# Dilated attention in an encoder layer: k copied on chip, statistics moved to VectorE, the join of head pairs placed later

## The chip, the cores and the metric

The kernel runs on one core of one Trainium2 chip. The metric is the device time of one execution in microseconds. Engines go by the profile's names: PE (TensorE, the matrix engine), DVE (VectorE), ACT (ScalarE), POOL (GpSimd) and SP (SyncE, which here issues the DMAs).

## The reference

One encoder layer, float32, run for a prompt of 256 tokens and a sample of 1024 tokens with shared weights:

```python
x = x + 0.5 * rms_norm(swiglu(rms_norm(x, g1), w_gu, w_down), g2)
x = x + rms_norm(mixer(rms_norm(x, g3)), g4)
x = x + 0.5 * rms_norm(swiglu(...))     # second feed-forward
x = rms_norm(x, final_g)

# mixer: [q|k|v|ga|gb] = h @ w_in, 8 heads of 64
outs, lses = [], []
for window, dilation in ((128, 1), (512, 4), (2048, 16)):
    o, lse = dilated_branch(q, k, v, slopes, dilation, window // (2 * dilation))
    outs.append(o); lses.append(lse)
w = softmax(stack(lses), axis=0)
attn = sum(w[..., None] * stack(outs), axis=0)
c = silu(layer_norm(depthwise_conv31(ga * sigmoid(gb))))
return concatenate([attn, c]) @ w_out
```

## The kernel before

Matrix products work on pairs (hi, lo): a value is rounded to float32r, and the rest is kept as a second tile. The program runs the first feed-forward, the mixer's input projection `w_in` with the convolution, the attention, the output projection `w_out`, and the second feed-forward. The projection writes q, k and v to DRAM (`qd`, `kd`, `vd`), and `attn` loads them head by head. `qd` and `kd` hold a hi and a lo part; a tile `q` has hi in partitions 0 to 63 and lo in 64 to 127, so k has to stand twice: `kH` and `kL` each hold the same 64 rows in both halves, loaded by four DMAs per head (L802). Buffers for q, k, v are two; heads alternate.

A head has nine groups (`qk_group`, two 128 x 256 blocks of scores each): four "classes" (tokens 4i + c of the sample, c = 0 to 3, which carry the branches of dilation 4 and 16), the prompt (group 4), and four of the near band of the sample, for which q is rearranged by `cast_qb` on POOL (L807). For each block DVE adds a table and takes the row minimum (L858), ACT takes the exponential and the row sum (L864); both go into the statistics tile `st` ("ast"). `next_tab` scales the tables for the next head (L823 on DVE, L825 on POOL). `t_group` transposes the probabilities on PE (L935), `evac` copies them out of the PSUM banks on ACT or DVE (L931, L929), and `pv_group` multiplies by v (L963). The score blocks, the transposes and the small products share four PSUM banks.

The class part and the band part of the sample are then merged by their statistics:

- `merge1` gathers the class statistics into the band's layout: 16 copies of 32 x 4 values on POOL (L884), from one quarter of the partitions to another.
- `merge2` takes the common minimum (L892 to L894, DVE), `merge3` exponentials (L897, ACT), `merge4` the factors (L902 to L907, DVE).
- `merge5` transposes the factors (L912), writes them to DRAM (`fd`, L917) and reads them back broadcast over 64 partitions (`x`, L924): four DMAs on SP.
- After each odd head, two heads are joined: `combine1` multiplies both parts (`t`: tiles "to" or "tmp") by the factors on POOL (L1013), and `combine2` adds them: POOL writes the rounded sum to `hT` (L1022), then DVE writes the sum over one of the inputs (L1023) and takes the rest (L1024).
- The prompt's result is rounded by ACT (L984), its rest taken by DVE (L985).

The loop's index `i` runs over all (head, group) pairs; `when(k, g, f)` calls f(h) k steps after group g of head h. Transposes lag four steps behind the scores and products with v two more. The order in which Python issues instructions is their priority; the framework then orders each engine's instructions itself from a model of when they become ready, so one that is issued later may stand earlier in an engine's queue. Each engine works through its queue in order, SP's queue of DMAs too.

The last two steps of the attention already fetch and round the weights of `w_out`, whose products (tiles `pso`) follow; L206 to L212 are the first steps of the norm after them.

Of the kernel before, what the change touches and what calls it, by code (L numbers as in the profile page):

```python
# [10 lines left out]
F32 = mybir.dt.float32  # L11
F32R = mybir.dt.float32r
AF = mybir.ActivationFunctionType
# [15 lines left out]
NH = 8  # L29
HD = 64  # L30
# [118 lines left out]
class Trunk:  # L149
# [624 lines left out]
    def attn(self, qk, pool, rpool, qd, kd, vd, after):  # L774
        nc = self.nc
        mm = nc.tensor.matmul
        H = {}

        KW = 288
        bufs = []  # L780
        for i in range(2):
            q = qk[i].tile([P, NT], F32R, name=f"q{i}")
            qb = qk[i].tile([P, NS], F32R, name=f"qb{i}")
            k = [qk[i].tile([P, 5, KW], F32R, name=f"k{z}{i}") for z in "HL"]
# [10 lines left out]
        def load_qk(h):  # L795
            d = H.setdefault(h, {})
            q, qb, k, d["v"] = bufs[h % 2]
            f = slice(h * HD, (h + 1) * HD)
            for i in range(2):
                nc.sync.dma_start(q[i * HD:(i + 1) * HD].bitcast(F32), qd[i, f, :])  # L800
            for z, o, s in ((0, 0, 0), (0, HD, 0), (1, 0, 1), (1, HD, 1)):
                nc.sync.dma_start(k[z][o:o + HD, :, 16:16 + 256].bitcast(F32), kd[s, f, :].rearrange("f (c i) -> f c i", c=5))  # L802
            d["q"], d["qb"], d["k"] = q, qb, k

        def cast_qb(h):
            q, qb = bufs[h % 2][0:2]
            nc.gpsimd.tensor_copy(qb.rearrange("p (b c j) -> p b c j", b=8, c=4),  # L807
                                  q[:, 0:NS].rearrange("p (c b j) -> p b c j", b=8, c=4).bitcast(F32))

        def load_v(h):  # L810
            o = h % 2 * HD
            v = bufs[h % 2][3][:, :, o:o + HD]
            vh = vd[:, :, h * HD:(h + 1) * HD]
            for c in range(5):
                nc.sync.dma_start(v[:, 2 * c:2 * c + 2, :], vh[c, 16:272, :].rearrange("(b p) d -> p b d", p=P))
            for c in range(4):
                nc.sync.dma_start(v[c * 32:(c + 1) * 32, 10:19, :], vh[c].rearrange("(j i) d -> i j d", i=32))
# [60 lines left out]
        def merge1(h):  # L878
            d = H[h]
            d["X"] = pool.tile([P, 8, 2], F32, name="ax", tag="ax", bufs=2)  # L880
            x = d["X"].rearrange("p (h r) s -> p h r s", h=2)
            for c in range(4):
                for r in range(4):
                    nc.gpsimd.tensor_copy(x[c * 32:(c + 1) * 32, :, r, :],  # L884
                                          d["st"][r * 32:(r + 1) * 32, 4 * c:4 * c + 4].rearrange("p (h s) -> p h s", s=2))

        def merge2(h):
            d = H[h]
            y = d["y"] = pool.tile([P, 4, 8], F32, name="ay", tag="ay", bufs=2)
            z = d["B"] = d["st"][:, 20:36].rearrange("p (b s) -> p b s", s=2)  # L890
            v = nc.vector.tensor_tensor
            v(y[:, 3], d["X"][:, :, 0], z[:, :, 0], op=OP.min)  # L892
            v(y[:, 0], y[:, 3], d["X"][:, :, 0], op=OP.subtract)
            v(y[:, 1], y[:, 3], z[:, :, 0], op=OP.subtract)  # L894
# [47 lines left out]
        def t_group(h, g):  # L942
            d = H[h]
            ps = self.bank("pst")
            k = GROUPS[g]
            if g < 5:
                for kb in range(2):
                    for i in range(2):
                        tr(ps, kb * 256 + i * P, d["P"][2 * g + i][:, kb * P:(kb + 1) * P])
            elif g == 6:  # L950
                tr(ps, 0, band(h, 6, 1))
                tr(ps, P, band(h, 6, 0))
                tr(ps, 256, band(h, 0, 0))
                tr(ps, 384, band(h, 8, 1))
            else:
                for i, j in enumerate(k):
                    tr(ps, i * 256, band(h, j, 1))
                    tr(ps, i * 256 + P, band(h, j, 0))
            d["T", g] = evac(g, ps)


        def pv(out, d, blk, T, c0, n, first, last):
            mm(out, d["v"][:, blk, :], T[:, c0:c0 + n], start=bool(first), stop=bool(last))  # L963

        def pv_group(h, g):
            d = H[h]
            T = d.pop(("T", g))
            kt, odd = divmod(h, 2)
            if g < 4:
                if g == 0:  # L970
                    d["OB"] = H[h - 1]["OB"] if odd else self.two_banks("ob")
                out = d["OB"][:, g * 256:(g + 1) * 256]
                for kb in range(2):
                    pv(out, d, 2 * g + kb, T, kb * 256, 256, not odd and g % 2 == 0 and kb == 0, odd and g % 2 == 1 and kb == 1)
                if g == 3 and odd:
                    d["t"] = [pool.tile([P, NS], F32, name="to", tag="to", bufs=2) if h % 4 == 1 else self.tmp("tmp") for _ in range(2)]
                    nc.scalar.activation(d["t"][1], d["OB"], AF.Copy)
            elif g == 4:
                o = slice(odd * HD, (odd + 1) * HD)
                op = self.bank("op")[:, 0:256]  # L980
                for kb in range(2):
                    pv(op, d, 8 + kb, T, kb * 256, 256, kb == 0, kb == 1)
                hi, lo = (z[o, kt, :] for z in self.hT[2])
                nc.scalar.activation(hi, op[o], AF.Copy)  # L984
                nc.vector.tensor_tensor(lo, op[o], hi.bitcast(F32), op=OP.subtract)  # L985
            else:
                if g == 5:
                    d["OA"] = H[h - 1]["OA"] if odd else self.two_banks("oa")
                oa = d["OA"]

                def two(j, c0):
                    a, z = (j - 1) * P, (j + 1) * P
                    if j == 4:
                        pv(oa[:, a:a + P], d, 10 + j, T, c0, P, False, False)
                        pv(oa[:, a + P:z], d, 10 + j, T, c0 + P, P, not odd, False)
                    else:
                        pv(oa[:, a:z], d, 10 + j, T, c0, 256, not odd and j == 2, odd and j in (3, 7))
                if g == 6:
                    two(6, 0)
                    pv(oa[:, 0:P], d, 10, T, 256, P, False, False)  # L1000
                    pv(oa[:, 7 * P:8 * P], d, 18, T, 384, P, False, False)
                else:
                    for i, j in enumerate(GROUPS[g]):
                        two(j, i * 256)
                if g == 8 and odd:
                    nc.scalar.activation(d["t"][0].rearrange("p (c b j) -> p c b j", c=4, b=8),
                                         oa.rearrange("p (b c j) -> p c b j", b=8, c=4), AF.Copy)
# [7 lines left out]
        def combine2(h):  # L1015
            d = H[h]
            if h % 2:
                ta, tb = d["t"]
                for t in range(2):
                    c = slice(t * 512, (t + 1) * 512)  # L1020
                    hi, lo = (z[:, h // 2, :] for z in self.hT[t])
                    nc.gpsimd.tensor_tensor(hi, ta[:, c], tb[:, c], op=OP.add)  # L1022
                    nc.vector.tensor_tensor(ta[:, c], ta[:, c], tb[:, c], op=OP.add)  # L1023
                    nc.vector.tensor_tensor(lo, ta[:, c], hi.bitcast(F32), op=OP.subtract)  # L1024

# [3 lines left out]
        load_v(0)  # L1029
        load_qk(1)  # L1030
        load_v(1)
        cast_qb(0)
        cast_qb(1)

        def at(i):
            return seq[i] if 0 <= i < len(seq) else (-1, -1)

        for i in range(len(seq) + LAG + LAG2 + 11):
            def when(k, g, f):
                h, gg = at(i - k)  # L1040
                if gg == g and h >= 0:
                    f(h)

            hq, gq = at(i)
            ht, gt = at(i - LAG)
            hv, gv = at(i - LAG - LAG2)
            if ht >= 0:
                t_group(ht, gt)
            when(5, 8, merge5)
            when(3, 8, merge3)  # L1050
            if hq >= 0:
                qk_group(hq, gq)
            when(2, 4, prompt_norm)
            when(1, 8, merge1)
            when(2, 8, merge2)
            when(4, 8, merge4)
            when(8, 8, lambda h: cast_qb(h + 2) if h + 2 < NH else None)
            when(13, 8, combine2)
            if hv >= 0:
                pv_group(hv, gv)  # L1060
                if gv == 8 and hv + 2 < NH:
                    load_v(hv + 2)
            if hq >= 0:
                exp_group(hq, gq)
                after.get((hq, gq), lambda: None)()
            when(10, 8, combine1)


    def w_out(self, S, base, stages, new_hT):
# [247 lines left out]
```

## Time and profile before

| | |
|---|---|
| median of three runs | 2363.11 us (2356.36 to 2365.82) |
| the profiled execution | 2363.5 us, its span 2361.7 us |
| mean granted PE clock | 0.987 |
| busy: PE, weight loads, DVE, ACT, POOL | 2287.1, 1958.5, 1277.8, 809.4, 674.1 us |
| the attention loop (first to last product of scores) | 1199.5 to 1348 us |

A row of a timeline gives the start in us, the duration in us, the engine, the line, the operation, what it writes and reads, and in brackets for how long the engine was idle before it and what ended that. A row of a group of instructions gives busy us and the mean in ns, then the idle time before them and what ended most of it. A row of windows gives the stretch, its length, busy us of PE, weight loads, DVE, ACT and POOL with counts, then the granted clock, the DMA share and GB/s.

### The profile page before, as it was taken

How to read it: one execution, taken by the hardware profiler on the slowest of the kernel's cores; microseconds unless marked ns; L12 is line 12 of the kernel's file. 1: busy time of each engine (PE TensorE's matmuls, PEld its weight loads, DVE VectorE, ACT ScalarE, POOL GpSimd, SP SyncE). 2: the span in 40 equal slices, each digit the busy share in tenths (PEclk: the TensorE clock that was granted, in tenths of full speed). 3: DMA queues.
4: the chain of work that ended last, by engine and by line, in shares of the span. 5: the costliest groups of instructions: out<-in, count | busy, mean ns of one | idle time of the engine just before them, and what ended most of it. 6: DMA issues, size and time to landing. Idle time of an engine off the chain costs nothing.

```text
span 2361.7 us, 30596 instructions
## 1 busy us (share of the span) xinstructions
PE 2287.1 (97%) x11788; PEld 1958.5 (83%) x11788; DVE 1277.8 (54%) x1796; ACT 809.4 (34%) x1530; POOL 674.1 (29%) x702
## 2 busy tenths in 40 slices
PE   7999999999999999999998999999999999999996
PEld 6888888888788887888887878888888888788885
DVE  5744343444454567998466833834444444545457
ACT  4322222223221234665377722322222222312123
POOL 2332232321000034897125443223233232000004
PEclk8999999999999999999999999999999999999998
DMA  4222212214332333341279642122221222423224
GB/s 158 63 64 63 79 63 70 76 59 130 96 100 79 104 111 125 96 117 49 97 162 173 159 132 98 52 79 63 70 72 63 70 76 77 156 74 94 85 80 154
DMA packets 209240, 223.51 MB, mean 95 GB/s; under 512 B 31012, under 2 KB 161060, under 8 KB 209094
## 3 DMA queue, kind: packets, MB, share of 16 engines
q1 hardware_dynamic: 209094, 221.56, 31.6%
q8 instruction: 92, 1.51, 0.3%
q14 instruction: 54, 0.44, 0.1%
HBM read 163.52 MB, written 58.00 MB: 94 GB/s over the span
## 4 chain that ended last, share of the span: by engine, by line
PE 88%; DVE 3%; DMA 3%; issue 2%; ACT 2%; POOL 2%; SPq 0%; POOLq 0%; ACTq 0%; DVEq 0%
PE psAB L198 8%; PE psAB L199 8%; PE psAB L200 8%; PE psd L198 7%; PE psd L199 7%; PE psd L200 7%; PE psR L199 3%; PE psR L200 3%; PE psR L198 3%; PE psC L198 3%; PE psC L199 3%; PE psC L200 3%; PE psgu L198 2%; PE psgu L199 2%; PE psgu L200 2%
## 5 line engine op out<-in xcount | busy, mean ns | idle before, releaser
L115 DVE TENSOR_TENSOR wb<-raw,wb 128x512 fp32r<-128x512 f32 x240 | 167.2, 698 | 218.6 <-ACT wb L114 213.9
L114 ACT ACTIVATE wb<-raw 128x512 fp32r<-128x512 f32 x240 | 150.7, 629 | 325.4 <-PE psAB L200 134.9
L207 POOL TENSOR_SCALAR st<-st 128x1 f32<-128x1 f32 x70 | 40.9, 584 | 638.0 <-ACT tmp L206 364.7
L198 PE MATMUL psd<-wd,ahl 128*128 128x512 f32 x500 | 197.6, 395 | 9.4 <-ACT y L563 3.8
L452 POOL TENSOR_TENSOR ac<-ac,tmp 128x512 f32<-128x512 f32 x40 | 67.4, 1685 | 464.0 <-DVE tmp L448 452.6
L199 PE MATMUL psd<-wd,ahl 128*128 128x512 f32 x500 | 196.0, 392 | 0.0
L200 PE MATMUL psd<-wd,ahl 128*128 128x512 f32 x500 | 195.9, 392 | 0.0
L534 ACT ACTIVATE ahl<-ar 128x512 fp32r<-128x512 f32 (+1 forms) x132 | 72.9, 556 | 351.8 <-PE psd L200 251.5
L199 PE MATMUL psR<-hT2l,wb 128*128 128x256 f32 x640 | 181.1, 283 | 0.0
L200 PE MATMUL psR<-hT2h,wb 128*128 128x256 f32 x640 | 180.9, 283 | 0.0
L198 PE MATMUL psR<-hT2h,wb 128*128 128x256 f32 x640 | 180.5, 282 | 0.0
L114 ACT ACTIVATE wb<-g 128x512 fp32r<-128x512 f32 x80 | 50.6, 632 | 224.9 <-POOL g L136 96.5
L198 PEld LDWEIGHTS psR<-hT2h,wb 128*128 128x128 f32 x640 | 122.2, 191 | 6.1
L199 PEld LDWEIGHTS psR<-hT2l,wb 128*128 128x128 f32 x640 | 122.2, 191 | 4.7
L198 PE MATMUL psAB<-hT0h,wb 128*128 128x512 f32 x320 | 125.7, 393 | 0.0
L198 PE MATMUL psC<-hT1h,wb 128*128 128x512 f32 x320 | 125.5, 392 | 0.0
L199 PE MATMUL psAB<-hT0l,wb 128*128 128x512 f32 x320 | 125.5, 392 | 0.0
L199 PE MATMUL psC<-hT1l,wb 128*128 128x512 f32 x320 | 125.4, 392 | 0.0
L200 PE MATMUL psAB<-hT0h,wb 128*128 128x512 f32 x320 | 124.5, 389 | 0.0
L200 PE MATMUL psC<-hT1h,wb 128*128 128x512 f32 x320 | 124.5, 389 | 0.0
L565 DVE TENSOR_TENSOR y<-y,psd 128x1024 f32<-128x1024 f32 x70 | 85.3, 1219 | 71.2 <-PE psd L200 71.2
L200 PEld LDWEIGHTS psR<-hT2h,wb 128*128 128x128 f32 x640 | 122.2, 191 | 1.6
(388 smaller groups left out, 6284.9 us busy)
## 6 DMA issues: line engine op xcount, KB each, us to landing
raw<-in_ffn_w_gu_dram SPq DMA_DIRECT2D x88, 512.0 KB
ad<-ac SPq DMA_DIRECT2D x88, 256.0 KB
g<-in_ffn_w_down_dram SPq DMA_DIRECT2D x44, 512.0 KB
ar<-ad SPq DMA_DIRECT2D x88, 256.0 KB
raw<-in_w_in_dram SPq DMA_DIRECT2D x20, 512.0 KB
ar<-ad SPq DMA_DIRECT2D x44, 128.0 KB
ad<-x SPq DMA_DIRECT2D x40, 128.0 KB
x2d<-y SPq DMA_DIRECT2D x10, 512.0 KB
```

The costliest lines, as they stand in the source:

```text
L114: nc.scalar.activation(out[:, 0], src, AF.Copy)
L115: nc.vector.tensor_tensor(out[:, 1], src, out[:, 0].bitcast(F32), op=OP.subtract)
L198: mm(out, lh[0], rh[0], start=first, stop=False, skip_group_check=more)
L199: mm(out, lh[0], rh[1], start=False, stop=False, skip_group_check=more)
L200: mm(out, lh[1], rh[0], start=False, stop=last, skip_group_check=more)
L207: nc.gpsimd.tensor_scalar(st[:, 0:1], st[:, 0:1], 1e-6 / (mul * mul), None, op0=OP.add)
L452: nc.gpsimd.tensor_tensor(a1, a1, q, op=OP.mult)
L534: nc.scalar.activation(hl[0], r, AF.Copy)
L565: nc.vector.tensor_tensor(y[b], y[b], o, op=OP.add)
```

## The change

Five things are edited, all inside `attn`. k's hi and lo are loaded into the lower 64 partitions only, by two DMAs instead of four, and the new `double_k` copies them to the upper 64 on POOL, just ahead of the same head's `cast_qb`. The copies of `merge1` go to DVE, and are issued one step later, together with `merge2`. The rounding of the prompt's result goes from ACT to DVE. `merge5` is issued one step later. `combine1` comes at 11 steps instead of 10; `combine2` is cut in two: the POOL part comes at 14 steps instead of 13, the DVE part (`combine3`) at 17. For the last head the three stay at 10, 13 and 13.

```diff
-            for z, o, s in ((0, 0, 0), (0, HD, 0), (1, 0, 1), (1, HD, 1)):
-                nc.sync.dma_start(k[z][o:o + HD, :, 16:16 + 256].bitcast(F32), kd[s, f, :].rearrange("f (c i) -> f c i", c=5))
+            for z in range(2):
+                nc.sync.dma_start(k[z][0:HD, :, 16:16 + 256].bitcast(F32), kd[z, f, :].rearrange("f (c i) -> f c i", c=5))
...
+        def double_k(h):
+            for z in bufs[h % 2][2]:
+                nc.gpsimd.tensor_copy(z[HD:, :, 16:16 + 256], z[0:HD, :, 16:16 + 256].bitcast(F32))
...
         def merge1(h):
...
-                    nc.gpsimd.tensor_copy(x[c * 32:(c + 1) * 32, :, r, :],
+                    nc.vector.tensor_copy(x[c * 32:(c + 1) * 32, :, r, :],
...
-                nc.scalar.activation(hi, op[o], AF.Copy)
+                nc.vector.tensor_copy(hi, op[o])
                 nc.vector.tensor_tensor(lo, op[o], hi.bitcast(F32), op=OP.subtract)
...
                     nc.gpsimd.tensor_tensor(hi, ta[:, c], tb[:, c], op=OP.add)
+
+        def combine3(h):
+            if h % 2:
+                ta, tb = H[h]["t"]
+                for t in range(2):
+                    c = slice(t * 512, (t + 1) * 512)
+                    hi, lo = (z[:, h // 2, :] for z in self.hT[t])
                     nc.vector.tensor_tensor(ta[:, c], ta[:, c], tb[:, c], op=OP.add)
                     nc.vector.tensor_tensor(lo, ta[:, c], hi.bitcast(F32), op=OP.subtract)
...
+        double_k(0)
         cast_qb(0)
+        double_k(1)
         cast_qb(1)
...
+            def late(k, k_last, f):
+                for lag, hs in ((k, range(NH - 1)), (k_last, (NH - 1,))):
+                    h, gg = at(i - lag)
+                    if gg == 8 and h in hs:
+                        f(h)
...
-            when(5, 8, merge5)
+            when(6, 8, merge5)
...
-            when(1, 8, merge1)
-            when(2, 8, merge2)
+            when(2, 8, lambda h: (merge1(h), merge2(h)))
             when(4, 8, merge4)
-            when(8, 8, lambda h: cast_qb(h + 2) if h + 2 < NH else None)
-            when(13, 8, combine2)
+            when(8, 8, lambda h: (double_k(h + 2), cast_qb(h + 2)) if h + 2 < NH else None)
+            late(14, 13, combine2)
+            late(17, 13, combine3)
...
-            when(10, 8, combine1)
+            late(11, 10, combine1)
```

## The prediction

> **What bounds the kernel now.** I read the page's busy lines first, then the chain of waits through the attention stage, then the timelines of single engines there.
>
> ```profile
> span 2361.7 us, 30596 instructions
> PE 2287.1 (97%) x11788; PEld 1958.5 (83%) x11788; DVE 1277.8 (54%) x1796; ACT 809.4 (34%) x1530; POOL 674.1 (29%) x702
> PE 88%; DVE 3%; DMA 3%; issue 2%; ACT 2%; POOL 2%; SPq 0%; POOLq 0%; ACTq 0%; DVEq 0%
> ```
>
> The matrix engine (PE) sets the time: only its gaps can be won. The change touches nothing outside the attention loop, so I measure that loop by a mark that comes once a head: the first product of a head's prompt group, heads 1 to 7.
>
> ```profile
> 1226.59 0.47 PE L853 MATMUL pss<-kH,q 128*128 128x256 f32 x1
> 1242.81 0.47 PE L853 MATMUL pss<-kH,q 128*128 128x256 f32 x1
> 1258.96 0.47 PE L853 MATMUL pss<-kH,q 128*128 128x256 f32 x1
> 1284.16 0.47 PE L853 MATMUL pss<-kH,q 128*128 128x256 f32 x1
> 1302.27 0.47 PE L853 MATMUL pss<-kH,q 128*128 128x256 f32 x1
> 1319.59 0.47 PE L853 MATMUL pss<-kH,q 128*128 128x256 f32 x1
> 1341.41 0.47 PE L853 MATMUL pss<-kH,q 128*128 128x256 f32 x1
> ```
>
> The distances are 16.2, 16.2, 25.2, 18.1, 17.3 and 21.8 us. The first two heads run without a gap: 16.2 us a head, 1.80 us for each of its nine steps. The others lose 9.0, 1.9, 1.1 and 5.6: together 17.6 us. That is all that the loop's middle can give back, 0.75% of the time. Where the two large losses come from:
>
> ```profile
> 1245.22 1.74 SPq L917 DMA_DIRECT2D fd<-asb  x2
> 1255.61 4.70 POOL L1013 TENSOR_TENSOR to<-to,x 128x1024 f32<-128x1024 f32 x2 [7.45 <-DMA x<-fd]
> 1262.34 1.05 POOL L807 CAST qb<-q 128x1024 fp32r<-128x1024 f32 x1
> 1263.35 1.27 POOL L1022 TENSOR_TENSOR hT0h<-to 128x512 fp32r<-128x512 f32 x1
> 1264.65 1.73 DVE L1023 TENSOR_TENSOR to<-to 128x512 f32<-128x512 f32 x1 [6.80 <-POOL hT0h L1022]
> 1267.13 0.58 PE L853 MATMUL pss<-kH,qb 128*128 128x256 f32 x1 [5.12 <-DVE ast L858]
> 1265.00:1270.00 5.00, 2.87 (x11) 2.69 (x12) 5.00 (x13) 2.87 (x9) 4.51 (x14) 0.57 0.70 121
> ```
>
> First loss: the join of heads 0 and 1. GpSimd (POOL) waits for the factors (x from fd), multiplies (L1013), and only then adds (L1022). VectorE (DVE) had its own add L1023 next in its queue; it rewrites what L1022 reads and so waited 6.80 us, with the score minima of the next groups behind it. PE ran out of free score banks for 5.12 us, and then (last row, a 5 us window; its last three numbers are granted clock, DMA share and GB/s) got a clock of 0.57.
>
> ```profile
> 1327.58 4.66 POOL L1013 TENSOR_TENSOR to<-to,x 128x1024 f32<-128x1024 f32 x2 [5.74 <-issue]
> 1327.65 2.32 DVE L892 TENSOR_TENSOR ay<-ax,ast 128x8 f32<-128x8 f32 x1
> 1330.01 2.26 DVE L893 TENSOR_TENSOR ay<-ay,ax 128x8 f32<-128x8 f32 x1
> 1333.13 1.33 PE L963 MATMUL op<-pT,v 128*128 128x256 f32 x4 [3.79 <-ACT pT L931]
> 1332.21 2.13 POOL L825 TENSOR_SCALAR g<-g 128x768 f32<-128x768 f32 x1
> 1332.96 0.16 DVE L902 TENSOR_TENSOR ay<-ax,ay 128x8 f32<-128x8 f32 x1
> 1292.42 2.26 DVE L893 TENSOR_TENSOR ay<-ay,ax 128x8 f32<-128x8 f32 x1
> 1295.36 1.64 DVE L902 TENSOR_TENSOR ay<-ax,ay 128x8 f32<-128x8 f32 x1
> 1268.90 0.68 DVE L1023 TENSOR_TENSOR to<-to 128x512 f32<-128x512 f32 x1
> ```
>
> Second loss, and the small ones: VectorE's tiny adds of the statistics take 0.16 us, but 2.3 us each while GpSimd runs L1013. ScalarE's exponential (L897) waits for them, the copies pT queue behind it, and PE waits 3.79 us. So two-input work on both engines excludes itself. L902 at 1332.96 ran at its plain 0.16 under GpSimd's one-input L825.
>
> **The change, part by part.** How VectorE's delay becomes PE's loss I take from the three cases: 3.6 us of excess (1292 to 1297) cost 1.9, 4.3 (1327 to 1332) cost 5.6, 7.9 (6.80, and L1023's 1.73 against the 0.68 of its other half) cost 9.0. Some 2.5 us are free, the rest costs 1 to 2 us for each.
>
> *Later join.* Combine3 comes four steps later than L1023 did, 7.2 us. VectorE reached L1023 at 1257.85 (1264.65 - 6.80) and would reach it at 1265.05. GpSimd's L1022 ended at 1264.62. It moves by +1.8 (merge5, whose four DMAs bring the factors, and combine1 are one step later) and by +2.6 if the two new copies of k stand ahead of it as the cast L807 does: 1269.0. Against that stands the lighter DMA queue: from fd's issue to L1013 it is 10.4 us here, but 7.3 in the next pair:
>
> ```profile
> 1284.96 0.65 SPq L917 DMA_DIRECT2D fd<-asb  x2
> 1292.29 4.69 POOL L1013 TENSOR_TENSOR tmp<-tmp,x 128x1024 f32<-128x1024 f32 x2 [7.54 <-issue]
> ```
>
> so 0 to 3.1 us come back, and VectorE waits 0.9 to 4.0 us. I take 2.0, as half of k's traffic goes; with 1.1 for its own blocked add that is 3.1, costing 1.5. Of the 9.0, 7.5 are won (bounds 3 and 9). In the later pairs L1023 hardly waited, and four steps keep it so.
>
> *Multiplications a step later.* In pairs 3 and 5 L1013 starts about 1.8 us later against merge1 to merge4. It leaves merge2 and lands on merge4, whose six small operations follow merge2 within 3 us. The loss of 1.9, 1.1 and 5.6 (8.7 with rounding) can vanish, or both pairs can be hit like the second (11.3 + 1.1, a loss of 3.7 more). No row decides; I take the half, 4.4 won (-3.7 to 8.7).
>
> *Statistics on VectorE; ScalarE's copy.*
>
> ```profile
> L884 POOL COPY ax<-ast 32x4 f32<-32x4 f32 x128 | 31.2, 244 | 13.7 <-ACT pr L864 8.9
> L858 DVE CUSTOM_DVE_ANT_0 pr<-pss,g 128x256 f32<-128x256 f32 x144 | 55.2, 419 | 24.7 <-PE pss L854 24.4
> L984 ACT ACTIVATE hT2h<-op 64x256 fp32r<-64x256 f32 x8 | 3.0, 372 | 0.1
> L807 POOL CAST qb<-q 128x1024 fp32r<-128x1024 f32 x7 | 7.3, 1041 | 24.4 <-DMA q<-qd 21.7 <-PE psm L912 2.7
> L825 POOL TENSOR_SCALAR g<-g 128x768 f32<-128x768 f32 x7 | 15.0, 2141 | 7.9 <-DVE ast L858 7.9
> ```
>
> 16 copies a head leave GpSimd (3.9 us) and come to VectorE. No such copy runs there now; between 0.08 (back to back, half of L902's plain 0.16) and 0.244 each, it is 1.3 to 3.9 us a head. I take the 0.16: 2.6. The prompt copy of L984 adds about 0.35. Against these 2.9 stand VectorE's 24.4 / 8 = 3.1 us a head of waiting for PE. Cover enough, but not always in the right place: 0.2 a head, over 7 heads 1.5 lost (0 to 8.4, from (4.3 - 3.1) x 7). If the cover is gone, each microsecond costs one on PE.
>
> *k loaded once.* Per head two DMAs less (64 x 1280 x 4 bytes, 320 KB each), two GpSimd copies of 64 x 1280 more. By L807's rate one is 1.30 us; by L825's, 3.56. The first is a copy too, so I take 2.6 a head. The price is hidden if k stands before the head's first product. Head 7 (its loads, and its first product):
>
> ```profile
> 1308.82 1.09 SPq L800 DMA_DIRECT2D q<-qd  x2
> 1313.81 1.82 SPq L802 DMA_DIRECT2D kL<-kd  x2
> 1315.25 1.04 POOL L807 CAST qb<-q 128x1024 fp32r<-128x1024 f32 x1 [7.25 <-DMA q<-qd]
> 1327.59 0.36 PE L853 MATMUL pss<-kH,q 128*128 128x256 f32 x1
> ```
>
> q took 6.4 us to land; k, issued by 1315.63, lands near 1322.0, is doubled by 1324.6, and is needed at 1327.59: 3.0 us to spare. With the dear copies (7.1) it is 1.5 late. Head 4's loads of q and k queue on SP behind the postponed factors, up to 1.8 later, with two issues fewer ahead of the end; it needs the relief of the queue to be in time. Cost 0 (to 9, at 1.5 for six heads); queued behind a late copy on GpSimd are the cast L807, L825 and the joins.
>
> The first use, head 1, waits today:
>
> ```profile
> 1218.69 0.38 PE L854 MATMUL pss<-kL,q 128*128 128x256 f32 x1 [1.82 <-DMA kL<-kd]
> 1215.00:1220.00 5.00, 3.18 (x26) 2.85 (x25) 2.39 (x10) 2.62 (x10) 2.17 (x1) 1.00 1.24 195
> ```
>
> 0.64 MB less at 195 GB/s brings k 3.2 us earlier, the two copies take 2.6: 0 (2.2 won to 2.6 lost, from the copies alone).
>
> *Tail.* Only merge5 of head 7 moves, one step, with its four DMAs on SP; combine1 to 3 keep their place.
>
> ```profile
> 1379.21 1.28 DVE L212 SCALAR_TENSOR_TENSOR tmp<-pso,st,g 128x1024 f32<-128x1024 f32 x1 [1.70 <-POOL st L208]
> ```
>
> VectorE has 1.70 us idle before L212, which PE awaits next; 0.5 lost (0 to 1.8).
>
> *Sum.* 7.5 + 4.4 - 1.5 - 0.5 = 9.9 us. The profiled execution took 2363.5 (2361.7 and 1.8 around it), so 2353.6; its time is 0.4 above the median of the three runs, 2363.11. I predict 2353, 0.4% less.
>
> **The Trainium skill** ("SBUF — State Buffer", section "Who interferes with whom") says that GpSimd and VectorE share one port pair as an exclusive lock, which a VectorE copy in a two-port mode, or one with two SBUF inputs against a GpSimd reader, holds or waits for whole. L892 under L1013 agrees; L902, at 0.16 under the reading L825, does not. By that rule the sixteen copies meet every GpSimd instruction, and the result is the third rival.
>
> **Rivals.** *Everything goes.* The multiplications fall between the small adds and the join never waits: 2363.5 - 17.6 + 0.5 = 2346. For it: GpSimd sheds 3.9 us a head, and the queue is lighter. Against: L1013 still needs 4.7 us per pair, beside eight two-input operations of VectorE a head.
>
> *The join's wait stays.* GpSimd's adds come as late as VectorE's: the 9.0 are lost again, the rest as forecast: 2363.5 - 4.4 + 1.5 + 0.5 = 2361. For it: L807 stood ahead of L1022 already, and the copies of k may too. Against: 7.2 us of postponement exceed the 6.80.
>
> *Slower: VectorE becomes the loop's bound.* If each of its copies can be shut out by one-input GpSimd work, the two copies of k, L807 and L825 (2.6 + 1.04 + 2.14 = 5.8 us a head) delay it by half of that on average, 2.9. With 2.9 of own work and 3.1 idle, that is 2.7 x 7 = 19 lost, against 11.4 won elsewhere: 2371. It decides from 4.7 us of added VectorE time a head (3.1 + 11.4 / 7). For it: the 2.3 us adds; no VectorE copy lies under such an instruction now, so nothing excludes it. Against: L902.
>
> *Slower: k doubled late*, as priced: 9 us over six heads, with the copies ahead of the joins taking the 7.5 too: 2370.
>
> **Chances.** Forecast 0.42 (2348 to 2358), everything goes 0.26, the wait stays 0.20, VectorE bound 0.09, k late 0.03. About 0.5% (11.8 us) is what a measurement here tells from no change: faster means under 2351.3, all of the second case and a quarter of the first, 0.36; slower 0.12; the same 0.52. The range 2343 to 2367 leaves out the slower cases and a little on each side; the forecast's own is 2348 to 2358.
>
> **What would show it.** Right: marks 16.2 to 18 us apart throughout; no wait of L1023's successor above 3 us; the sixteen copies near 0.16 us each; no wait of L853 or L854 for GpSimd's k; the clock not below 0.9 in the middle. Wrong: a mark distance above 20, copies of 0.3 us and more beside GpSimd rows, PE waiting for k, or VectorE without idle time before L858.

## The result, and the profile after

The changed kernel takes 2384.27 us (median, 2381.62 to 2385.65) against 2362.44 for the kernel before: ratio 1.0094, 95% interval [1.0071, 1.0117]. It is 21.8 us slower; 2353 was forecast. First the page of the changed kernel: span, busy lines, and the chain of waits.

```profile
span 2383.0 us, 30633 instructions
PE 2297.7 (96%) x11788; PEld 1961.1 (82%) x11788; DVE 1310.0 (55%) x1932; ACT 806.1 (34%) x1522; POOL 664.0 (28%) x590
PE 87%; DVE 6%; ACT 2%; issue 2%; DMA 2%; POOL 2%; SPq 0%; POOLq 0%; ACTq 0%; DVEq 0%
```

VectorE (DVE) is busy 32 us longer than before and its share of the chain went from 3 to 6%. Now the marks of the prediction, from PE's timeline of the changed kernel: the first product of a head's prompt group, heads 1 to 7.

```profile
1225.68 0.36 PE L858 MATMUL pss<-kH,q 128*128 128x256 f32 x1
1244.82 0.36 PE L858 MATMUL pss<-kH,q 128*128 128x256 f32 x1
1267.67 0.58 PE L858 MATMUL pss<-kH,q 128*128 128x256 f32 x1 [1.00 <-DVE ast L863]
1287.81 0.47 PE L858 MATMUL pss<-kH,q 128*128 128x256 f32 x1
1313.88 0.36 PE L858 MATMUL pss<-kH,q 128*128 128x256 f32 x1
1334.35 0.36 PE L858 MATMUL pss<-kH,q 128*128 128x256 f32 x1
1359.34 0.36 PE L858 MATMUL pss<-kH,q 128*128 128x256 f32 x1
```

The distances are 19.1, 22.9, 20.1, 26.1, 20.5 and 25.0 us; no head runs at the clean 16.2 any more. From head 1 to head 7 it is 133.7 us against 114.8: 18.8 of the 21.3 us by which the span grew. So most of the loss lies where the prediction looked. The third distance alone is shorter than before (20.1 for 25.2), because GpSimd's part of the first join now falls into the second; the two together grew by 1.6 us, each of the four others by 2.9 to 8.0. Another 3.9 us lie behind the last mark: from it to the first product of `w_out` 13.8 us pass (1359.34 to 1373.11) for 9.9 before (1341.41 to 1351.27). The groups of VectorE's instructions in the attention stage (1198 to 1372 us) of the changed kernel:

```profile
L863 DVE CUSTOM_DVE_ANT_0 pr<-pss,g 128x256 f32<-128x256 f32 x144 | 54.0, 419 | 8.6 <-PE pss L859 7.9
L889 DVE COPY ax<-ast 32x4 f32<-32x4 f32 x128 | 29.4, 230 | 2.1
L989 DVE CAST hT2h<-op 64x256 fp32r<-64x256 f32 x7 | 2.9, 419 | 4.1 <-PE op L968 3.9
```

The minima (L863, the L858 of before) take the same 419 ns, but of the 24.7 us that VectorE stood idle ahead of them only 8.6 are left: two thirds of the cover are gone. The sixteen statistics copies a head (L889) fill 29.4 us, 3.7 a head, at a mean of 230 ns. Single rows of the changed kernel's timeline, around the first join, show what stretches them:

```profile
1244.13 0.67 DVE L889 COPY ax<-ast 32x4 f32<-32x4 f32 x4
1257.02 4.68 POOL L1018 TENSOR_TENSOR to<-to,x 128x1024 f32<-128x1024 f32 x2 [0.85 <-DMA x<-fd]
1258.19 4.83 DVE L889 COPY ax<-ast 32x4 f32<-32x4 f32 x4
1261.76 1.25 POOL L808 CAST kH<-kH 64x1280 fp32r<-64x1280 f32 x1
1264.28 1.28 POOL L1027 TENSOR_TENSOR hT0h<-to 128x512 fp32r<-128x512 f32 x1
1264.10 2.71 DVE L889 COPY ax<-ast 32x4 f32<-32x4 f32 x4
1263.62 0.36 PE L858 MATMUL pss<-kH,q 128*128 128x256 f32 x1 [2.86 <-DVE hT2l L990]
1260.00:1265.00 5.00, 2.14 (x16) 1.87 (x15) 4.88 (x8) 0.60 (x1) 4.85 (x4) 0.96 0.32 42
1265.00:1270.00 5.00, 4.00 (x14) 3.00 (x14) 4.75 (x19) 2.69 (x10) 1.78 (x2) 0.50 0.02 3
```

Alone, four copies take 0.67 us. Beside the rest of GpSimd's (POOL's) multiplications of the join and its copy of kH behind them, four take 4.83; beside its adds 2.71. Nine of the 128 copies take over 0.3 us, the others 0.15 to 0.17; the nine hold 8.8 us above the usual 0.16, and 6.2 of these fall on this one join. PE works 2.14 of the 5 us after 1260, and then has a granted clock of 0.50. A second thing shows in the same kernel, at head 2:

```profile
1224.01 1.25 POOL L808 CAST kH<-kH 64x1280 fp32r<-64x1280 f32 x1 [0.58 <-DMA kH<-kd]
1225.65 1.25 POOL L808 CAST kL<-kL 64x1280 fp32r<-64x1280 f32 x1 [0.39 <-DMA kL<-kd]
1236.28 0.37 PE L858 MATMUL pss<-kH,q 128*128 128x256 f32 x1
1241.42 0.36 PE L859 MATMUL pss<-kL,q 128*128 128x256 f32 x1
```

k of head 2 stood doubled at 1226.9. PE began with kH at 1236.28, but the first product with kL, which completes that block, came 5.1 us later, with no wait noted ahead of it: it stood there in PE's queue, behind other work. In the kernel before, 143 of the 144 products of kH were followed at once by their kL; in the changed one 128 are.

### The profile page after: what moved, and what is told of

It is laid out like the page before. It is cut to its first block, busy times and chain, and to the rows that moved or that the text cites. A ratio compares the mean times of both kernels' runs of the same rounds, so it can differ in the third digit from the quotient of the medians.

```text
span 2383.0 us, 30633 instructions
## 1 busy us (share of the span) xinstructions
PE 2297.7 (96%) x11788; PEld 1961.1 (82%) x11788; DVE 1310.0 (55%) x1932; ACT 806.1 (34%) x1522; POOL 664.0 (28%) x590
## 4 chain that ended last, share of the span: by engine, by line
PE 87%; DVE 6%; ACT 2%; issue 2%; DMA 2%; POOL 2%; SPq 0%; POOLq 0%; ACTq 0%; DVEq 0%
PE psAB L198 8%; PE psAB L199 8%; PE psAB L200 8%; PE psd L198 7%; PE psd L199 7%; PE psd L200 7%; PE psR L199 3%; PE psR L200 3%; PE psR L198 3%; PE psC L198 3%; PE psC L199 3%; PE psC L200 3%; PE psgu L198 2%; PE psgu L199 2%; PE psgu L200 2%
## 5 line engine op out<-in xcount | busy, mean ns | idle before, releaser
L198 PEld LDWEIGHTS psR<-hT2h,wb 128*128 128x128 f32 x640 | 122.2, 191 | 6.1
L198 PEld LDWEIGHTS psd<-wd,ahl 128*128 128x128 f32 x500 | 94.3, 189 | 35.7 <-ACT y L563 5.3
```

Of the source, the lines that this page charges most:

```text
L198: mm(out, lh[0], rh[0], start=first, stop=False, skip_group_check=more)
```

## The experiments

Two theories were set against each other. *VectorE*: the copies of the statistics on VectorE, shut out beside GpSimd, carry the loss. *Order*: the dependency of the products on GpSimd's copies of k gives PE's queue another order, blocks of scores come to VectorE in bursts, and PE stands idle between them. "Join" means that the later steps of the join cost it. Names: u_ takes one part of the change out again, o_ has one part alone on the kernel before, a_ keeps the whole change and edits one thing in it. "Over before" is the median less that of the kernel before on the same chip (2359.97 to 2362.88 us).

| run | over before, us | ratio, 95% interval |
|---|---|---|
| changed kernel | +21.8 | 1.0094 [1.0071, 1.0117] |
| u_stats | +12.3 | 1.0057 [1.0039, 1.0076] |
| u_double | +11.8 | 1.0051 [1.0034, 1.0068] |
| u_join | +20.7 | 1.0086 [1.0071, 1.0101] |
| u_stats_double | +1.3 | 1.0004 [0.9994, 1.0013] |
| o_stats | +9.6 | 1.0039 [1.0024, 1.0054] |
| o_stats_red | +2.6 | 1.0009 [1.0000, 1.0018] |
| o_double | +14.4 | 1.0064 [1.0048, 1.0080] |
| o_double_rev2 | +5.0 | 1.0025 [1.0015, 1.0036] |
| o_spare | +28.5 | 1.0125 [1.0109, 1.0141] |
| o_join | +3.9 | 1.0017 [1.0006, 1.0028] |
| o_tab | -1.0 | 0.9996 [0.9983, 1.0008] |
| o_join_tab | -0.8 | 0.9999 [0.9990, 1.0008] |
| o_prompt | +1.3 | 1.0008 [0.9999, 1.0017] |
| a_rev2 | +16.4 | 1.0073 [1.0051, 1.0095] |
| a_red | +10.1 | 1.0048 [1.0033, 1.0064] |
| a_fix | +9.5 | 1.0044 [1.0032, 1.0056] |
| u_stats_rev2 | +4.9 | 1.0023 [1.0011, 1.0034] |

**Which part.** Four runs take parts out or put one in.

u_stats, the changed kernel with the copies back on GpSimd:

```diff
-                    nc.vector.tensor_copy(x[c * 32:(c + 1) * 32, :, r, :],
+                    nc.gpsimd.tensor_copy(x[c * 32:(c + 1) * 32, :, r, :],
```

> The changed kernel with the sixteen copies of merge1 back on GpSimd, all else as changed. If VectorE's added work (29.4 us of copies, its idle time before L863 down from 24.7 to 8.6 us) makes the loss, most of it goes: 2355 to 2366 us. If the loss comes from the order of PE's products (the second product of a block held back behind the copy of k), it stays: 2375 us or more. If the later join is to blame: 2378 us or more.

u_double, the changed kernel with k loaded four times again:

```diff
-            for z in range(2):
-                nc.sync.dma_start(k[z][0:HD, ...
+            for z, o, s in ((0, 0, 0), (0, HD, 0), (1, 0, 1), (1, HD, 1)):
+                nc.sync.dma_start(k[z][o:o + HD, ...
...
-            when(8, 8, lambda h: (double_k(h + 2), cast_qb(h + 2)) if h + 2 < NH else None)
+            when(8, 8, lambda h: cast_qb(h + 2) if h + 2 < NH else None)
```

> The changed kernel with k loaded four times per head and no copies of k on GpSimd, all else as changed. VectorE theory: 2378 to 2386 us, the copies of merge1 still fill VectorE. Order theory: the products of a block stand together again and the marks of the heads come 17 us apart: 2360 to 2368 us.

u_join, the changed kernel with the join at its old steps:

```diff
-            when(6, 8, merge5)
+            when(5, 8, merge5)
-            late(14, 13, combine2)
-            late(17, 13, combine3)
-            late(11, 10, combine1)
+            when(13, 8, combine2)
+            when(13, 8, combine3)
+            when(10, 8, combine1)
```

> The changed kernel with merge5 and the three combines at the steps of before. Both the VectorE and the order theory: no better, 2380 to 2392 us, for the late join takes VectorE's waits away (L1023 waited 14 us before). If the later join were the cause: below 2370 us.

o_stats, the kernel before with the copies on VectorE:

```diff
-                    nc.gpsimd.tensor_copy(x[c * 32:(c + 1) * 32, :, r, :],
+                    nc.vector.tensor_copy(x[c * 32:(c + 1) * 32, :, r, :],
...
-            when(1, 8, merge1)
-            when(2, 8, merge2)
+            when(2, 8, lambda h: (merge1(h), merge2(h)))
```

> The kernel before with merge1 on VectorE and issued together with merge2, nothing else. VectorE theory: 2375 to 2390 us, as 2.75 us of copies a head plus their blocking by GpSimd's instructions exceed 3.1 us of idle time less the waits for the join. Order theory: within 5 us of 2362.

Measured: 2372.28, 2371.74, 2380.7 and 2369.6 us. Neither theory has it all. Taking out the copies gives back 9.5 us, taking out the doubling 10.0, the join next to nothing. A later run, u_stats_double, takes both out (the edits of u_stats and u_double, with merge1 issued together with merge2):

> The changed kernel without two of its parts: k loaded four times as before, statistics copies on GpSimd as before (issued together with merge2, one step later than before). Later join and the prompt's copy on VectorE remain. If the whole loss hangs on the two parts taken out, 2360 to 2367, as the sum of the runs of the other two alone would be (3.9 and 1.3 us over the kernel before). If join and prompt cost more together than alone, 2368 to 2374. The forecast's terms of the join would give 2351.

2364.13 us, 1.3 over before: these two parts carry the loss, and what is left costs nothing that can be told from zero. It brings nothing either.

**The copies: time or shut-out?** o_stats_red writes each copy of o_stats as a maximum over an axis of one element, on the same bytes:

```diff
-                    nc.vector.tensor_copy(x[c * 32:(c + 1) * 32, :, r, :],
-                                          d["st"][...].rearrange("p (h s) -> p h s", s=2))
+                    nc.vector.tensor_reduce(x[c * 32:(c + 1) * 32, :, r, :],
+                                            d["st"][...].rearrange("p (h s o) -> p h s o", s=2, o=1),
+                                            axis=mybir.AxisListType.X, op=OP.max)
```

> As the earlier run with the sixteen statistics copies a head on VectorE (2369.6 us), but each copy is written as a maximum over an axis of one element: the same bytes with another VectorE instruction. Theory 'the copies are shut out while GpSimd holds the shared port, as copies': the reductions run beside GpSimd's rows at their plain time, and the loss falls to what the own time costs, 2361 to 2366. Rival 'VectorE's own time and queueing': the loss stays, 2368 to 2375. If the reductions stretch beside GpSimd's multiplications like the copies did, the shut-out is not one of copies.

Measured: 2364.3 us, 2.6 over before where the copies cost 9.6. The group of the copies, the first join in the timeline, and an earlier stretch of o_stats:

```profile
L889 DVE COPY ax<-ast 32x4 f32<-32x4 f32 x128 | 35.1, 274 | 4.9 <-ACT pr L869 2.3
1222.50 1.04 POOL L812 CAST qb<-q 128x1024 fp32r<-128x1024 f32 x1 [6.23 <-PE psm L917]
1222.41 1.50 DVE L889 COPY ax<-ast 32x4 f32<-32x4 f32 x4 [0.29 <-ACT pr L869]
1252.04 4.67 POOL L1018 TENSOR_TENSOR to<-to,x 128x1024 f32<-128x1024 f32 x2 [15.41 <-DMA x<-fd]
1252.32 4.41 DVE L889 COPY ax<-ast 32x4 f32<-32x4 f32 x2
1259.45 0.58 PE L858 MATMUL pss<-kH,q 128*128 128x256 f32 x1 [4.45 <-DVE pT L934]
```

And of o_stats_red:

```profile
L889 DVE TENSOR_REDUCE ax<-ast 32x4 f32<-32x4 f32 x128 | 19.0, 149 | 5.0 <-ACT pr L869 2.4
1255.05 4.67 POOL L1019 TENSOR_TENSOR to<-to,x 128x1024 f32<-128x1024 f32 x2 [14.71 <-ACT pr L869]
1255.34 2.10 DVE L910 TENSOR_TENSOR ay<-ay 128x8 f32<-128x8 f32 x1
1257.36 0.30 DVE L889 TENSOR_REDUCE ax<-ast 32x4 f32<-32x4 f32 x2
1258.25 2.48 DVE L913 TENSOR_TENSOR ay<-ay 128x8 f32<-128x8 f32 x2
```

Two copies beside the join's multiplications take 4.41 us; two reductions beside the same multiplications take 0.30, while the two-input operations around them (L910, L913) are still held up. In the two traces each of PE, VectorE, ScalarE and GpSimd works through its instructions in the same order, so only the kind of the instruction differs. So 7.0 of the 9.6 us are the shut-out (less at most 1.5 for the reduction's shorter own time: 149 for 161 ns in the median, 128 times), and 2.6 the instructions' own time and place. It is not only two-input work that shuts copies out: beside the one-input cast of q (1.04 us) four copies took 1.50 instead of 0.67. The Trainium skill, "SBUF — State Buffer", section "Who interferes with whom", says that copies can enter the mode that takes the port pair shared with GpSimd, and that `tensor_reduce` never contends on this chip; both agree with 274 and 149 ns here: 33 reductions that lay wholly inside GpSimd instructions took 137 to 153 ns. But not all of a GpSimd instruction shuts copies out. Beside the scaling of the table (L830, 2.13 us) the copies of o_stats that began in its first 0.84 us ended when these were over, six that began 0.85 to 1.3 us into it ran at their usual 150 to 161 ns, and those that began 1.77 to 1.88 us into it waited for its end.

**The doubling: lateness, GpSimd's time, or order?**

o_double has `double_k` and its two loads alone on the kernel before.

> The kernel before with one part of the change: k is loaded into the lower 64 partitions only and copied up by GpSimd (two copies of 64 x 1280 a head). In the order of the instructions, 13 of the 144 products of kH are now not followed by their product of kL; in the kernel before it is 1. Theory 'order of the products': the score groups come to VectorE in clumps, 2368 to 2376 us, with second products held back in the trace though kL is long copied. Rival 'time on VectorE': the doubling costs nothing by itself, 2357 to 2365, and the other causes carry it.

o_double_rev2 is o_double with kL first:

```diff
-            for z in range(2):
+            for z in (1, 0):
                 nc.sync.dma_start(k[z][0:HD, ...
...
-            for z in bufs[h % 2][2]:
+            for z in bufs[h % 2][2][::-1]:
```

> As the run before, but kL is loaded and copied first and kH second, nothing else. By that alone every product of kH is again followed at once by its product of kL. GpSimd does the same copies for the same time. Theory 'order': the loss goes, within 4 us of the kernel before, 2356 to 2365. Rivals: if it is the copies' time on GpSimd (1.25 us each, ahead of the cast and the joins) or their lateness against the first product, the loss stays, 2368 to 2376.

o_spare, the kernel before with two more copies:

```diff
+        scr = qk[1].tile([P, 5, 256], F32R, name="scr")
+        def spare(h):
+            for z in bufs[h % 2][2]:
+                nc.gpsimd.tensor_copy(scr[HD:], z[0:HD, :, 16:16 + 256].bitcast(F32))
...
-            when(8, 8, lambda h: cast_qb(h + 2) if h + 2 < NH else None)
+            when(8, 8, lambda h: (spare(h + 2), cast_qb(h + 2)) if h + 2 < NH else None)
```

> The kernel before, k loaded four times as there, and besides it two GpSimd copies of 64 x 1280 a head into a scratch tile that nothing reads. No product waits for GpSimd. But the order of the products is changed as with the doubling: 12 of the 144 products of kH are not followed by their kL. Theory 'order': 2366 to 2376, though no data depends on the copies. Rival 'products wait for late copies of k': no loss, 2358 to 2366. By itself it does not tell the order from GpSimd's time; together with the run before it does.

Measured: 2376.11, 2366.67 and 2390.23 us. Swapping the two halves of k gives back 9.4 of the doubling's 14.4 us, with the same copies for the same time (means of 1.25 to 1.28 us), and in neither does PE wait for a copy of k. The swap changes the order of all engines' queues, not only that of the parted products (VectorE's first add of the join stands behind 75 minima instead of 80): the run shows that the order carries the 9.4 us; that the parted products do it is argued from what follows. What the order does is seen at head 4 of o_double, timeline rows of four engines and a window:

```profile
1259.64 1.25 POOL L808 CAST kL<-kL 64x1280 fp32r<-64x1280 f32 x1
1269.77 0.37 PE L858 MATMUL pss<-kH,q 128*128 128x256 f32 x1
1277.25 0.47 PE L859 MATMUL pss<-kL,q 128*128 128x256 f32 x1
1277.99 0.42 DVE L863 CUSTOM_DVE_ANT_0 pr<-pss,g 128x256 f32<-128x256 f32 x1 [3.04 <-PE pss L859]
1281.64 1.13 PE L968 MATMUL ob<-pT,v 128*128 128x256 f32 x4 [1.41 <-ACT pT L936]
1284.99 0.37 PE L917 MATMUL psm<-ident,ay 128*16 128x128 f32 x1 [2.21 <-DVE ay L912]
1280.00:1285.00 5.00, 1.38 (x8) 0.72 (x6) 4.42 (x19) 3.28 (x14) 3.44 (x11) 0.96 0.17 40
```

kL was copied by 1260.89; its first product stands at 1277.25, 7.5 us behind that of kH. VectorE stands idle for 3.04 us, then gets eight blocks in a row, with the join and the statistics behind them, and PE waits 1.41 and 2.21 us: busy 1.38 of 5 us. In o_double_rev2 the same two products lie 0.20 us apart:

```profile
1274.88 0.36 PE L858 MATMUL pss<-kH,q 128*128 128x256 f32 x1
1275.08 0.28 PE L859 MATMUL pss<-kL,q 128*128 128x256 f32 x1
```

o_spare did not isolate what it was meant to. The copies that nobody waits for were ordered late on GpSimd, and the next load of that buffer waited for them, so kL came late by DMA, as o_spare's group of the kL products and one row show:

```profile
L860 PE MATMUL pss<-kL,q 128*128 128x256 f32 x80 | 23.0, 322 | 17.5 <-DMA kL<-kd 17.5
1258.94 0.58 PE L860 MATMUL pss<-kL,q 128*128 128x256 f32 x1 [6.68 <-DMA kL<-kd]
```

The 17.5 us of waiting are a third mechanism; the run says nothing on the order.

**Both in the whole change.** a_rev2 is the changed kernel with the swap of o_double_rev2, a_red with the reductions of o_stats_red, a_fix with both.

> The changed kernel whole, with kL loaded and copied before kH, nothing else. All of its 144 products of kH are now followed at once by their kL (128 in the changed kernel). If the order of the products carries the loss of the doubling, 2369 to 2378, that is 8 to 14 us less than the changed kernel; what is left is the shut-out copies. If the changed kernel's loss is one of VectorE alone, 2380 to 2387.

> The changed kernel whole, each of the sixteen statistics copies written as a maximum over an axis of one element, nothing else. If the shut-out of the copies carries about 8 us, as before to o_stats and o_stats_red show, 2371 to 2379. If it is only VectorE's added time or another order of its queue, 2381 to 2387.

> The changed kernel with both edits: kL first, and the statistics as reductions. All four parts of the change stay. If the two causes are all of the loss and add up, 2358 to 2368, no different from the kernel before; by the first forecast's sum without them, 2353. If something of the change beyond the two costs time (join later, prompt's result on VectorE, GpSimd's copies), 2370 or more.

Measured: 2378.42, 2372.14 and 2371.5 us. The reductions give back 11.7 us, the swap 5.4 (its interval overlaps that of the changed kernel), both together 12.3. So the two do not add up here: with reductions the swap is worth 0.6, not to be told from zero. In a_rev2 the swap also brought more shut-out: the copies there took 270 ns in the mean instead of 230, 5.1 us in all. The shut-out is shown for the whole change; the order is shown on the kernel before, and in the whole change only as a tendency. a_fix is on the side that was written "2370 or more": something beyond the two causes costs time, 9.5 us.

**What stays, and the join.** u_stats_rev2 is u_stats with the swap. o_prompt has the prompt's rounding alone on VectorE:

```diff
-                nc.scalar.activation(hi, op[o], AF.Copy)
+                nc.vector.tensor_copy(hi, op[o])
```

> The changed kernel with the statistics copies back on GpSimd and kL loaded and copied first: k doubled, prompt's result on VectorE and later join remain, without the two causes found. If the 9 us that the changed kernel keeps with kL first and reductions (2371.5) are VectorE's own added time of the sixteen instructions, 2360 to 2366. If they are of the join, the prompt's copy and the doubling on GpSimd, 2368 to 2374.

> The kernel before with the upper part of the prompt's result copied out of its bank by VectorE instead of ScalarE; nothing else. Theory: 0.35 us a head more on VectorE, the same less on ScalarE, 2360 to 2365, not to be told from the kernel before. Rival: VectorE's instruction waits for PE's bank with minima queued behind it, at every head, and 2366 to 2371 comes out; then this is a third cause of the changed kernel's loss.

Measured: 2367.01, between the two ranges, and 2363.46 us. Against u_stats (12.3 over before) the swap gives back 7.4 us, and the two intervals do not overlap: with the statistics on GpSimd the order counts beside the rest of the change too. From a_fix to u_stats_rev2 4.5 us go (the intervals just overlap): the sixteen instructions on VectorE, even when nothing shuts them out. The 4.9 that are left are about what o_double_rev2 has (5.0). By these differences a_fix's rest is half VectorE's own time and half the doubling in its better order; it is an account, not a test. What the latter half consists of stays open: PE waits for no copy of k in either.

The join, alone on the kernel before (the last hunks of the change), and with GpSimd's halving of the second table on ScalarE:

```diff
-                nc.gpsimd.tensor_scalar(tab[1], tab[1], 0.5, None, op0=OP.mult)
+                nc.scalar.activation(tab[1], tab[1], AF.Copy, scale=0.5)
```

> The kernel before with only the later join: merge5 and combine1 one step later, the second half of combine2 split off and four steps later. The forecast's term: 7.5 us won in the join of heads 0 and 1 and up to 4.4 in the others, 2350 to 2356. Rival: the wait of 6.80 us goes but PE's gap is taken by the small operations of the statistics, which now meet GpSimd's multiplications: 2358 to 2366.

> The kernel before with GpSimd's halving of the second table (2.14 us, once a head) on ScalarE instead. Control for the next run. In the kernel before no instruction waits long for that table: 2357 to 2365. If GpSimd's time as such sets the loop, 2350 to 2356.

> The later join alone, as in o_join (2365.9 us), with the halving of the second table on ScalarE as in the run before. In o_join's trace the multiplications of the join stood ahead of the halving on GpSimd, and VectorE's minima waited 3.68 us for the table. Theory 'the join's wait was exchanged for one for the table': without it the later join gains what was forecast for heads 0 and 1, 2350 to 2358. Rival 'the gain is lost in the small operations and in the halves of the join itself, whatever GpSimd does': 2361 to 2368.

Measured: 2365.88, 2361.17 and 2361.39 us. The later join alone loses 3.9 us instead of winning 7.5; without the table on GpSimd it is level with o_tab. The first join in o_join's timeline:

```profile
1262.47 3.08 POOL L1018 TENSOR_TENSOR to<-to,x 128x1024 f32<-128x1024 f32 x1
1265.52 2.12 POOL L830 TENSOR_SCALAR g<-g 128x768 f32<-128x768 f32 x1
1267.60 2.76 POOL L889 COPY ax<-ast 32x4 f32<-32x4 f32 x12
1267.67 0.42 DVE L863 CUSTOM_DVE_ANT_0 pr<-pss,g 128x256 f32<-128x256 f32 x1 [3.68 <-POOL g L830]
1268.60 0.37 PE L858 MATMUL pss<-kH,qb 128*128 128x256 f32 x1 [2.37 <-DVE ast L863]
1271.74 1.75 DVE L1035 TENSOR_TENSOR to<-to 128x512 f32<-128x512 f32 x1 [2.08 <-POOL hT0h L1027]
```

and in o_join_tab's:

```profile
1262.42 1.28 POOL L1027 TENSOR_TENSOR hT0h<-to 128x512 fp32r<-128x512 f32 x1
1263.73 1.73 DVE L1035 TENSOR_TENSOR to<-to 128x512 f32<-128x512 f32 x1 [3.74 <-POOL hT0h L1027]
1266.93 0.65 PE L940 MATMUL pst<-ident,pr 128*128 128x128 f32 x4 [3.24 <-DVE ast L863]
```

In o_join the multiplications came later, the halving of the table stood behind them, and VectorE's minima waited 3.68 us for the table; PE lost 2.37 instead of 5.12. Where the 3.9 us lie, this one execution shows in part: its marks of heads 1 to 7 span 113.9 us, 0.9 less than before, but the third join's add, which waited for nothing before (1338.68), now comes behind the mark of head 7, at 1343.80 after 1.88 us of waiting, and from that mark to the first product of `w_out` 12.8 us pass instead of 9.9. In o_join_tab that wait is gone, but VectorE reached its add at 1259.99 and waited 3.74 us for GpSimd after all. In the instruction order the first L1035 stands behind 68 minima in o_join and behind 62 in o_join_tab, the 62 of the kernel before: the framework had put the "later" add back where it was. So o_join_tab takes away both the table and the later place, and that the table alone makes the loss is not shown. No version tried is faster than the kernel before by more than its interval.

## Why the prediction was wrong, point by point

- **The bound** held: PE sets the time, its gaps lie in the attention loop, and VectorE's delays make them. 18.8 of the 21.3 us of the span are between the marks of heads 1 and 7.
- **Statistics on VectorE**, -1.5 (bounds 0 to 8.4): the mechanism left out of the sum was the one that came. The plain price was right (0.17 us a copy for the 0.16 taken), the own time too: 16 x 0.17 = 2.7 us a head for 2.6. But the copies took 230 ns in the mean, and alone on the kernel before they cost 9.6 us, beyond the bound; 7.0 of that is the shut-out. The failing step is "Against: L902", which gave the third rival only 0.09: one two-input add that ran freely, begun 0.75 us into L825, was taken as evidence on copies. The trace before had rows that say otherwise of L825 itself, from head 1's statistics:

```profile
1234.29 2.14 POOL L825 TENSOR_SCALAR g<-g 128x768 f32<-128x768 f32 x1 [4.54 <-DVE ast L858]
1234.65 0.48 DVE L892 TENSOR_TENSOR ay<-ax,ast 128x8 f32<-128x8 f32 x1
```

L892 took 0.48 us instead of 0.16 and ended 0.85 us after L825's start, as the copies of o_stats did beside the same instruction. By the rule quoted there, which the prediction set aside, the copies wait for GpSimd's instructions whole. The runs agree beside the multiplications, the adds, the cast and the copies of k; beside the table's scaling they wait in a part of it only.
- **That rival's price** (2371) was 19 lost on VectorE against 11.4 won elsewhere. u_double, with the shut-out and without the doubling, is at 2371.74, but by another sum: the copies alone cost 9.6 (o_stats), and no run shows the 11.4 won. That the number fits is luck.
- **k loaded once**, 0 (to -9): the copies were priced right (1.25 us for 1.30), and PE never waited for one. What failed is that the cost of a dependency was looked for only as a wait. It came as an order: 14.4 us alone, 9.4 of them undone by swapping kH and kL; the other 5.0 stay open.
- **Later join**, +7.5: both delays in this term were mis-sized. VectorE's add was taken as four steps, 7.2 us, later; but a step in the loop's text is a priority, not a place in VectorE's queue: in o_join 68 minima stand ahead instead of 62, three steps, and without the table none more. GpSimd's add was taken as 1.8 us later without the copies of k; in o_join it ended at 1271.71 instead of 1264.62, 5.5 us later when measured from the mark of head 2, for the table's halving and twelve statistics copies stood ahead of it. Measured alone the later join costs 3.9 us, though beside the prompt's copy (u_stats_double) the two together cost 1.3. In the changed kernel the wait of 6.80 us did go (the first L1035 starts at 1284.63 without one), but u_join, which undoes the later join, is no slower (1.1 us faster, within the intervals). (By the prediction's own rule 3.1 us of delay would have cost 0.6 to 1.2, not 1.5.)
- **Multiplications a step later**, +4.4: not won. u_stats_double and o_join hold this edit and are at or over the kernel before; its own share was not measured. That four steps keep the later pairs free of waits did not hold either: the adds of the second and third pair, which waited 0.18 us at most before, wait 1.32 and 1.88 us in o_join. The last pair's waited 7.29 us even before (1372.53, behind the loop).
- **Prompt and first use**: 0.42 us a head on VectorE for the 0.35 taken, 1.3 us in the time, which the interval does not tell from zero. PE's wait of 1.82 us for kL at the first use is gone; what that is worth was not measured. **Tail**, -0.5: not measured by itself, but the sum had nothing for the third join, which the later steps put behind the last mark; that stretch grew by 3.9 us in the changed kernel and 2.9 in o_join.
- Of the signs named for "wrong", three came: mark distances above 20, copies above 0.3 us beside GpSimd rows, VectorE's idle time before the minima down to a third. The fourth, PE waiting for k, did not.

## What to carry to other kernels

Before a small copy is moved to VectorE, look at what GpSimd does in the same microseconds: the copy's price can be not its plain duration but the rest of GpSimd's instruction, and the same move written as a reduction (149 against 274 ns here) kept clear of it. Where a framework orders the queues, a new dependency or a later step changes the order even where no wait shows, so compare the orders before pricing an edit, and look for operands that stand ready long before their use. Ask of every removed wait which instruction stands next in that queue, and of every postponed one what is queued behind it.

## What was not expected of the hardware

- Small VectorE copies were held up by GpSimd work with one input too: four in 1.50 instead of 0.67 us beside a 1.04 us cast. Beside the table's scaling of 2.13 us it was the first 0.84 us and the end that held them up, not the stretch between.
- Copies out of the PSUM banks were not held up: that of `pT` at 1263.40 in the changed kernel took 0.67 us wholly inside GpSimd's copy of kL (1262.95 to 1264.20).
- A reduction over one element moved 32 x 4 values across partition quarters in 0.15 us, faster than the copy's 0.17, and stood free beside multiplications that held up copies and two-input adds for over 2 us.
- Loading half of k took the transfers from 223.5 to 218.3 MB, and no run with it is faster than its counterpart without.
